# adaLN in a two-layer diffusion block: sums of two column blocks and both conditions on four column parts of TensorE, and the steps around a SwiGLU chunk's end dealt out anew

## The chip, the cores and the metric

The kernel runs on one core of a Trainium2 chip. The metric is the device time of one execution in microseconds, median of several runs. The profile is one further execution; its times count from the first instruction. Engines: PE (TensorE, matmuls; PEld its weight loads), DVE (VectorE), ACT (ScalarE), POOL (GpSimd), SP (SyncE, which here only issues transfers).

## The reference, cut to what matters

```python
def reference(x, c, ctx, c_ctx, ...):          # x 512 x 1024, ctx 256 x 1024
    for i in range(2):
        mod = silu(c) @ w_ada[i] + b_ada[i]        # 1024 -> 6 * 1024, latent tokens
        mod_c = silu(c_ctx) @ w_ada[i] + b_ada[i]  # the same, context tokens
        sh1, sc1, g1, sh2, sc2, g2 = split(mod, 6)
        h = rms_norm(x, norm_mix[i]) * (1 + sc1) + sh1
        y = short_conv(h) if i == 0 else neighbourhood_attention(h, hc)
        x = x + g1 * y
        x = x + g2 * swiglu(rms_norm(x, norm_ffn[i]) * (1 + sc2) + sh2)
        # layer 0 does the same to ctx with mod_c; layer 1 reads ctx and does not update it
    return x

def swiglu(h):                                 # hidden width 2816
    gate, up = split(h @ w_in, 2)
    return (silu(gate) * up) @ w_out
```

Everything is float32. The modulation needs, for each layer, the product of one vector (latent) and, where context is still used, of a second one (context) with a 1024 x 6144 matrix.

## The kernel before

Features lie on the 128 partitions and tokens along the free axis: x is eight tiles of 128 x 512, the context eight of 128 x 256. A product with float32 accuracy is three matmuls: weights and activations are each split into a high and a low part (fp32r), and hi x hi, hi x lo and lo x hi are summed (`mm3`, L186 to L210; its matmuls have line L192). `split` (L136) makes the parts: ACT converts to the high part (L138: wh, ah), DVE subtracts to get the low part (L139: wl, al). `Stream` (L146) loads blocks of 256 weight columns into `raw` and splits them one item ahead of use. `raw` has three buffers, and the blocks of w_ada take theirs from the same three.

The modulation of the columns that the first norm does not need is done by the class `Ada` in the shadow of the big products. Its unit is a step: one half (512 rows) of one block of 512 columns of w_ada. A step loads 1 MB into `raw` (L277) and sums its four 128-row slices, each times its entries of silu(c), into an accumulator `aa` of 128 x 512. For the latent condition DVE does this (L290 the first slice, L292 the others); for the context condition ACT multiplies (L295 the first slice, L298 the others into `pr`) and POOL adds (L299). The context condition is needed for all of layer 0's blocks and for the first four of layer 1's. There are 40 steps; four of them, two column blocks, make one flush: PE sums the accumulators over the 128 partitions (L313), ACT copies the sums from PSUM to `row` (L319), PE transposes them (L322), and DVE adds the bias into `mod` (L328). So there are ten flushes, six with both conditions and four with one.

In the sums of a flush, the column block sets the column part: block j goes to output partitions 32j to 32j + 31. `ones2` holds, for each condition, 32 columns of which one is 1 and the rest 0; the two conditions are accumulated into the same part, one after the other, and come out on two of its rows.

The SwiGLU of layer 0 (`swiglu`, L470) goes through the hidden width in chunks of 6, 8 and 8 tiles. For each hidden tile PE makes gate and up products of x, then of the context; `gate` (L485) forms sg (L489) and splits it into ah and al. Behind the tiles of a chunk comes its output product (`residual`, L449): for each output tile f = 0 to 7 a product over the chunk's hidden tiles for x (18 matmuls in chunk 0) and one for the context (18), each followed by the residual add on DVE (L444). Steps are placed by code: one behind each hidden tile (L551), and in chunks 0 and 1 one behind each of f = 0, 2, 4 of the output product (`also`: flush if four steps are done, then a step), with a flush behind f = 6 (L556).

The order of instructions on each engine is made by a scheduler from estimated times, within the dependences and with the matmuls of sums and transposes pinned in the order of the program. Each engine then runs its own queue in order and waits on semaphores; so an instruction of a step can stand, in DVE's queue, ahead of one that the code wrote earlier.

Of the kernel before, what the change touches and what calls it, by code (L numbers as in the profile page):

```python
# [9 lines left out]
F32 = mybir.dt.float32  # L10
F32R = mybir.dt.float32r
AF = mybir.ActivationFunctionType
ALU = mybir.AluOpType
AX = mybir.AxisListType

P = 128
# [22 lines left out]
def dit_kernel(  # L39
# [16 lines left out]
    nc = tc.nc  # L56
    const = ctx.enter_context(tc.tile_pool(name="const", bufs=1))
# [23 lines left out]
    ident = ct[:, C_ID:C_ID + P]  # L81
# [4 lines left out]
    nc.vector.tensor_copy(out=sel, in_=sel_raw)  # L86
    ones = const.tile([P, 32], F32, name="ones")
    nc.vector.memset(ones, 1.0)
    ones2 = const.tile([P, 2, 32], F32, name="ones2")
    nc.vector.memset(ones2, 0.0)  # L90
    nc.vector.memset(ones2[:, 0, 0:1], 1.0)
    nc.vector.memset(ones2[:, 1, 1:2], 1.0)
    eps = const.tile([P, 1], F32, name="eps")
    nc.vector.memset(eps, EPS)
    pick = const.tile([P, 4], F32, name="pick")
# [26 lines left out]
    def in_order(inst):  # L122
        return tc.keep_in_program_order(inst)
# [89 lines left out]
    class Ada:  # L213
# [90 lines left out]
        def flush(self):  # L304

            if len(self.todo) < 2:
                return
            two, self.todo = self.todo, []
            i, q, both, _ = two[0]
            self.ps = bank("ada", "ada_ps")  # L310
            for c in range(1 + both):
                for j, (_, _, _, accs) in enumerate(two):
                    in_order(nc.tensor.matmul(self.ps[32 * j:32 * j + 32, :], ones2[:, c, :], accs[c],  # L313
                                              start=(c == 0), stop=(c == both)))
            self.finish(i, q // 2)

        def finish(self, i, g):
            row = nrm.tile([P, 512], F32, name="row", tag="row", bufs=1)
            nc.scalar.copy(out=row[0:64, :], in_=self.ps[0:64, :])  # L319
            tp = bank("ada", "ada_tp")  # L320
            for s in range(4):
                in_order(nc.tensor.transpose(out=tp[:, s * 64:(s + 1) * 64], in_=row[0:64, s * P:(s + 1) * P],  # L322
                                             identity=ident[0:64, 0:64]))
            tv = tp[:, 0:256].rearrange("p (s j m) -> p j s m", s=4, j=2)
            ba = vt[:, V_BADA + i * 48 + g * 8:V_BADA + i * 48 + g * 8 + 8].rearrange("p (j s) -> p j s", j=2)
            conds = range(2 if i == 0 or g < 2 else 1)
            for cond in conds:
                nc.vector.tensor_tensor(  # L328
                    out=mod[i][:, cond, g * 8:g * 8 + 8].rearrange("p (j s) -> p j s", j=2),
                    in0=tv[:, :, :, cond], in1=ba, op=ALU.add)  # L330
            if g not in (1, 4):
                return
            which = 0 if g == 1 else 1
            base = V_NMIX if which == 0 else V_NFFN
            gt = const.tile([P, 2, KT], F32, name=f"gain{i}{which}")
            for cond in conds:
                nc.vector.scalar_tensor_tensor(
                    out=gt[:, cond, :], in0=mod[i][:, cond, g * 8:g * 8 + 8], scalar=1.0,
                    in1=vt[:, base + i * KT:base + (i + 1) * KT], op0=ALU.add, op1=ALU.mult)
            gains[(i, which)] = gt  # L340
# [129 lines left out]
    def swiglu(tmp, ap_, i, groups, hs, chunks, ada=None, begin=None, norms=None, out=None, end=None, begin_norm=None):  # L470
# [3 lines left out]
        for ci, n_t in enumerate(chunks):  # L474
            for pr in range(n_t // 2):
                c = (t0 + 2 * pr) * P
                g = block(((ci, pr), "g"), w_in, 0, KT, c)
# [18 lines left out]
        for ci, n_t in enumerate(chunks):  # L496
            srcs = [([], []) for _ in groups]
            tt = 0
            if ci == 0 and begin is not None:
                ws = [st.next() for _ in range(2)]  # L500
                pss, prev = {}, {}

                def in_turn(g):

                    for m in mm3_steps.begun if g in prev else ():
                        behind(m, prev[g])
                    prev[g] = mm3_steps.last

                for g, sub, hooks, hooks3 in begin:
                    c0, c1 = sub.c0, sub.c0 + sub.n  # L510
                    if g not in pss:
                        pss[g] = [bank("mm", "ps") for _ in range(3)]
                    mm3_steps.pin_all = g == 0 and sub.n == NX
                    if len(groups) > 1 and g == 1:
                        begin_norm.apply(hs[1])
                    for part in (((0, 1),) if hooks else ((0,), (1,))):
                        mm3([pss[g][p][:, c0:c1] for p in part], [ws[p] for p in part], *sub.of(hs[g]), hooks)
                    mm3_steps.pin_all = False
                    in_turn(g)
                    if c1 == groups[g].n:  # L520
                        gate(g, pss[g][0], pss[g][1], srcs)
                    if c0 == 0:
                        if len(ws) < 3:
                            ws.append(st.next())
                        grp = groups[g]
                        if grp.n == sub.n:
                            mm3([pss[g][2][:, :grp.n]], [ws[2]], *grp.of(hs[g]), hooks3)
                if begin[0][1].n < groups[0].n:
                    mm3([pss[0][2]], [ws[2]], *groups[0].of(hs[0]))
                if ada is not None:  # L530
                    ada.flush()
                wu = st.next()
                for g, grp in enumerate(groups):
                    pu = bank("mm", "ps")
                    mm3([pu[:, :grp.n]], [wu], *grp.of(hs[g]))
                    gate(g, pss[g][2], pu, srcs)
                tt = 2
                if ada is not None:
                    ada.step(2)
            while tt < n_t:  # L540
                wg, wu = st.next(), st.next()
                for g, grp in enumerate(groups):
                    pg, pu = bank("mm", "ps"), bank("mm", "ps")
                    hi, lo = grp.of(hs[g])
                    mm3([pg[:, :grp.n]], [wg], hi, lo)
                    if ada is not None and g == 0 and tt > 2:
                        ada.flush()
                    mm3([pu[:, :grp.n]], [wu], hi, lo)
                    gate(g, pg, pu, srcs)
                if ada is not None:  # L550
                    ada.step()  # L551
                tt += 1
            last = ci == len(chunks) - 1
            if last and end is not None:
                norms, out = end()
            along = {0: ada.also, 2: ada.also, 4: ada.also, 6: ada.flush} if ada is not None and not last else None  # L556
            residual(st, i, 5, groups, srcs, norms if last else None, out, along=along)


# [1 line left out]
    with ExitStack() as l0:  # L561
# [6 lines left out]
        ada = Ada(tmp, cs)  # L568
# [157 lines left out]
    with ExitStack() as l1:  # L726
# [200 lines left out]
        last, norms = [], []  # L927
# [155 lines left out]
```

## Time and profile before

| | us |
|---|---|
| median of 3 runs | 1640.12 (1639.3 to 1641.58) |
| the profiled execution | 1639.04 |
| its span, first to last instruction | 1637.2 |
| PE busy | 1607.5 (98%) |
| DVE busy | 859.5 (52%) |
| ACT busy | 578.3 (35%) |
| POOL busy | 242.9 (15%) |

1.84 us of the profiled execution lie outside its span. A matmul's row in the timeline gives start and modelled duration, and matmuls are pipelined: the distance between starts, not the duration, is what one costs. The granted clock is 0.998 of full speed over the span. A float32 matmul of the sums is two rows in the trace (two passes).

### The profile page before, as it was taken

The numbers are of one execution on the slowest core, as the hardware profiler recorded it, in microseconds if no ns is written. First come the engines' busy times: TensorE is split into PE (matmuls) and PEld (weight loads), VectorE is DVE, ScalarE is ACT, GpSimd is POOL, SyncE is SP. The second block draws the span as 40 slices with busy tenths as digits, with TensorE's granted clock in tenths as the row PEclk, the third lists the DMA queues.
The fourth block names the chain that finished last, engine by engine and source line by source line (L and its number), as shares of the span: only waits on it lengthen the run. The fifth ranks groups of instructions, "written<-read, shape, count | busy, mean of one in ns | idle before, by whom it ended". The sixth has DMA issues, their size and how long they took to land.

```text
span 1637.2 us, 22217 instructions
## 1 busy us (share of the span) xinstructions
PE 1607.5 (98%) x9156; PEld 1344.5 (82%) x9156; DVE 859.5 (52%) x1393; ACT 578.3 (35%) x967; POOL 242.9 (15%) x290
## 2 busy tenths in 40 slices
PE   6999999999999999999999999999999999999998
PEld 5898888788888888888888777777778788888887
DVE  5567667476654534344423766655677533333333
ACT  4243234354323221122222555555555422222221
POOL 0123226324422000000013201111111000000000
PEclk9999999999999999999999999999999999999999
DMA  9424343134433425133421201111122222323221
GB/s 314 137 78 130 103 154 117 64 122 130 135 127 105 140 93 180 54 127 104 154 68 42 84 27 59 33 59 32 47 71 78 77 98 83 100 81 128 78 84 71
DMA packets 137222, 162.43 MB, mean 99 GB/s; under 512 B 3232, under 2 KB 114208, under 8 KB 137120
## 3 DMA queue, kind: packets, MB, share of 16 engines
q1 hardware_dynamic: 133504, 156.66, 29.4%
q10 hardware_dynamic: 3616, 4.34, 0.8%
q8 instruction: 72, 1.18, 0.3%
q14 instruction: 30, 0.25, 0.0%
HBM read 158.90 MB, written 2.10 MB: 98 GB/s over the span
## 4 chain that ended last, share of the span: by engine, by line
PE 93%; DVE 3%; ACT 1%; DMA 1%; issue 1%; POOL 0%; SPq 0%; POOLq 0%; DVEq 0%; ACTq 0%
PE ps L192 83%; PE op L908 2%; PE tp L898 2%; PE ada_ps L240 1%; PE s L878 1%; DMA raw<-in_w_ada_dram 1%; PE ada_ps L313 1%; PE s L879 1%; PE stt L795 1%; DVE wl L139 1%; DVE t L428 0%; DVE aa L292 0%; PE bc L412 0%; DVE hxl L431 0%; DMA x<-in_xT_dram 0%
## 5 line engine op out<-in xcount | busy, mean ns | idle before, releaser
L192 PE MATMUL ps<-hxh,wh 128*128 128x512 f32 (+1 forms) x1128 | 435.4, 392 | 3.5 <-ACT hxh L430 1.7
L192 PE MATMUL ps<-hxl,wh 128*128 128x512 f32 (+1 forms) x1128 | 431.8, 388 | 1.3 <-DVE hxl L431 1.1
L192 PE MATMUL ps<-hxh,wl 128*128 128x512 f32 (+1 forms) x1128 | 431.1, 388 | 0.5 <-DVE wl L139 0.5
L138 ACT CAST wh<-raw 128x1024 fp32r<-128x1024 f32 (+1 forms) x194 | 198.1, 1022 | 471.4 <-PE ps L192 424.8
L139 DVE TENSOR_TENSOR wl<-raw,wh 128x1024 fp32r<-128x1024 f32 (+1 forms) x194 | 242.1, 1249 | 172.8 <-ACT wh L138 169.0
L192 PEld LDWEIGHTS ps<-hxh,wh 128*128 128x128 f32 x1128 | 210.5, 188 | 53.3 <-issue 4.1
L192 PEld LDWEIGHTS ps<-hxh,wl 128*128 128x128 f32 x1128 | 211.8, 188 | 45.1 <-DVE wl L139 1.4
L192 PEld LDWEIGHTS ps<-hxl,wh 128*128 128x128 f32 x1128 | 211.2, 188 | 43.5 <-DVE hxl L431 3.2
L192 PE MATMUL ps<-ah,wh 128*128 128x512 f32 (+1 forms) x656 | 232.3, 354 | 2.7 <-ACT ah L138 2.7
L192 PE MATMUL ps<-al,wh 128*128 128x512 f32 (+1 forms) x656 | 231.8, 354 | 0.3 <-DVE al L139 0.3
L192 PE MATMUL ps<-ah,wl 128*128 128x512 f32 (+1 forms) x656 | 230.9, 352 | 0.0
L192 PE MATMUL ps<-hch,wl 128*128 128x256 f32 x648 | 181.3, 284 | 0.0
L192 PE MATMUL ps<-hcl,wh 128*128 128x256 f32 x648 | 180.5, 283 | 0.0
L192 PE MATMUL ps<-hch,wh 128*128 128x256 f32 x648 | 179.8, 284 | 0.0
L292 DVE SCALAR_TENSOR_TENSOR aa<-raw,cs,aa 128x512 f32<-128x512 f32 x140 | 144.5, 1033 | 40.9 <-DMA raw<-in_w_ada_dram 37.8
L299 POOL TENSOR_TENSOR aa<-aa,pr 128x512 f32<-128x512 f32 x84 | 135.0, 1608 | 184.3 <-ACT pr L298 111.4
L192 PEld LDWEIGHTS ps<-ah,wh 128*128 128x128 f32 x656 | 123.7, 189 | 25.1 <-issue 3.7
L192 PEld LDWEIGHTS ps<-al,wh 128*128 128x128 f32 x656 | 123.8, 189 | 18.3 <-DVE al L139 0.6
L192 PEld LDWEIGHTS ps<-ah,wl 128*128 128x128 f32 x656 | 123.9, 189 | 17.5
L444 DVE SCALAR_TENSOR_TENSOR x<-ps,mod,x 128x512 f32<-128x512 f32 (+1 forms) x80 | 55.2, 695 | 140.4 <-PE ps L192 140.2
L192 PEld LDWEIGHTS ps<-hch,wh 128*128 128x128 f32 x648 | 122.1, 191 | 4.4 <-issue 1.9
L192 PEld LDWEIGHTS ps<-hcl,wh 128*128 128x128 f32 x648 | 122.8, 191 | 1.9
(172 smaller groups left out, 1595.6 us busy)
## 6 DMA issues: line engine op xcount, KB each, us to landing
raw<-in_ffn_w_in_dram SPq DMA_DIRECT2D x44, 1024.0 KB, 5.1
raw<-in_w_ada_dram SPq DMA_DIRECT2D x40, 1024.0 KB, 5.2
raw<-in_ffn_w_out_dram SPq DMA_DIRECT2D x16, 1024.0 KB, 5.1
raw<-in_attn_w_qkv_dram SPq DMA_DIRECT2D x12, 1024.0 KB, 5.2
raw<-in_conv_w_in_dram SPq DMA_DIRECT2D x9, 1024.0 KB, 5.2
raw<-in_w_ada_dram SPq DMA_DIRECT2D x16, 512.0 KB, 7.9
raw<-in_ffn_w_out_dram SPq DMA_DIRECT2D x8, 768.0 KB, 4.6
raw<-in_conv_w_out_dram SPq DMA_DIRECT2D x4, 1024.0 KB, 5.2
```

What stands on the lines that cost most here:

```text
L138: a = pinned(nc.scalar.copy(out=hi, in_=src))
L139: b = pinned(nc.vector.tensor_tensor(out=lo, in0=src, in1=hi.bitcast(F32), op=ALU.subtract))
L192: m = nc.tensor.matmul(ps, w[k][part], src[k], start=(first and k == i == 0), stop=(last and k == nk - 1 and i == 2))
L240: in_order(nc.tensor.matmul(self.ps[32 * j:32 * j + 32, :wd], self.cs[:, k, :], raw[:, kk, j // 2, j % 2 * wd:(j % 2 + 1) * wd], start=(k ...
L292: nc.vector.scalar_tensor_tensor(out=acc, in0=raw[:, kk, :], scalar=w, in1=acc, op0=ALU.mult, op1=ALU.add)
L299: nc.gpsimd.tensor_tensor(out=acc, in0=acc, in1=pr, op=ALU.add)
L313: in_order(nc.tensor.matmul(self.ps[32 * j:32 * j + 32, :], ones2[:, c, :], accs[c], start=(c == 0), stop=(c == both)))
L444: nc.vector.scalar_tensor_tensor(out=grp.tiles[f], in0=ps, scalar=modv(i, grp.cond, gate, f), in1=grp.tiles[f], op0=ALU.mult, op1=ALU.add)
L795: nc.tensor.matmul(stt[row:row + 32, :], ind, sq, start=True, stop=True)
L878: nc.tensor.matmul(s, qh[a][:, bs], keys(ks[a], w0), start=True, stop=False)
L898: nc.tensor.transpose(out=tp[:, j * P:(j + 1) * P], in_=pt[:, c0:c0 + P], identity=ident)
L908: in_order(nc.tensor.matmul(op_[own, 0:P], vv[:, vi, own], tps[a][:, j * P:(j + 1) * P], start=(j == 0), stop=(j == 3)))
```

## The change

Three things. The sums of a flush go to a column part of their own for each block and condition (four parts with both conditions, two with one), with the plain `ones` as weights and without accumulating; `ones2` and its three memsets go. With both conditions the copy and the four transposes then take 128 rows instead of 64, and the bias add reads the first row of each part. Last, in chunks 0 and 1 the step behind the last hidden tile goes, and the output product has four steps, behind f = 0, 1, 3 and 5, instead of three behind 0, 2 and 4; the last chunk keeps the step behind each tile, and the number and order of steps stay.

```diff
--- before.py
+++ after.py
@@ -86,10 +86,6 @@
     nc.vector.tensor_copy(out=sel, in_=sel_raw)
     ones = const.tile([P, 32], F32, name="ones")
     nc.vector.memset(ones, 1.0)
-    ones2 = const.tile([P, 2, 32], F32, name="ones2")
-    nc.vector.memset(ones2, 0.0)
-    nc.vector.memset(ones2[:, 0, 0:1], 1.0)
-    nc.vector.memset(ones2[:, 1, 1:2], 1.0)
     eps = const.tile([P, 1], F32, name="eps")
     nc.vector.memset(eps, EPS)
     pick = const.tile([P, 4], F32, name="pick")
@@ -308,26 +304,25 @@
             two, self.todo = self.todo, []
             i, q, both, _ = two[0]
             self.ps = bank("ada", "ada_ps")
-            for c in range(1 + both):
-                for j, (_, _, _, accs) in enumerate(two):
-                    in_order(nc.tensor.matmul(self.ps[32 * j:32 * j + 32, :], ones2[:, c, :], accs[c],
-                                              start=(c == 0), stop=(c == both)))
+            for r, acc in enumerate(acc for _, _, _, accs in two for acc in accs):
+                in_order(nc.tensor.matmul(self.ps[32 * r:32 * r + 32, :], ones, acc, start=True, stop=True))
             self.finish(i, q // 2)
 
         def finish(self, i, g):
             row = nrm.tile([P, 512], F32, name="row", tag="row", bufs=1)
-            nc.scalar.copy(out=row[0:64, :], in_=self.ps[0:64, :])
+            nr = P if i == 0 or g < 2 else P // 2
+            nc.scalar.copy(out=row[0:nr, :], in_=self.ps[0:nr, :])
             tp = bank("ada", "ada_tp")
             for s in range(4):
-                in_order(nc.tensor.transpose(out=tp[:, s * 64:(s + 1) * 64], in_=row[0:64, s * P:(s + 1) * P],
-                                             identity=ident[0:64, 0:64]))
-            tv = tp[:, 0:256].rearrange("p (s j m) -> p j s m", s=4, j=2)
+                in_order(nc.tensor.transpose(out=tp[:, s * nr:(s + 1) * nr], in_=row[0:nr, s * P:(s + 1) * P],
+                                             identity=ident[0:nr, 0:nr]))
+            tv = tp[:, 0:4 * nr].rearrange("p (s j c m) -> p j s c m", s=4, j=2, m=32)
             ba = vt[:, V_BADA + i * 48 + g * 8:V_BADA + i * 48 + g * 8 + 8].rearrange("p (j s) -> p j s", j=2)
             conds = range(2 if i == 0 or g < 2 else 1)
             for cond in conds:
                 nc.vector.tensor_tensor(
                     out=mod[i][:, cond, g * 8:g * 8 + 8].rearrange("p (j s) -> p j s", j=2),
-                    in0=tv[:, :, :, cond], in1=ba, op=ALU.add)
+                    in0=tv[:, :, :, cond, 0], in1=ba, op=ALU.add)
             if g not in (1, 4):
                 return
             which = 0 if g == 1 else 1
@@ -547,13 +542,13 @@
                         ada.flush()
                     mm3([pu[:, :grp.n]], [wu], hi, lo)
                     gate(g, pg, pu, srcs)
-                if ada is not None:
+                if ada is not None and (tt < n_t - 1 or ci == len(chunks) - 1):
                     ada.step()
                 tt += 1
             last = ci == len(chunks) - 1
             if last and end is not None:
                 norms, out = end()
-            along = {0: ada.also, 2: ada.also, 4: ada.also, 6: ada.flush} if ada is not None and not last else None
+            along = {0: ada.also, 1: ada.step, 3: ada.also, 5: ada.also, 6: ada.flush} if ada is not None and not last else None
             residual(st, i, 5, groups, srcs, norms if last else None, out, along=along)
```

DVE's queue at the end of chunk 0. First the kernel before: `raw_3971` is the block of the step at f = 0, `raw_4079` that of the step at f = 2 (w_ada); `raw_3789` and `raw_3989` are blocks of w_out for f = 0, 1 and f = 2, 3; sg_3845, al0_3849 belong to the last hidden tile's x columns, sg_3902, al1_3906 to its context columns.

```order
L290 TENSOR_SCALAR aa0_3973<-raw_3971,cs_116 128x512
L292 SCALAR_TENSOR_TENSOR aa0_3973<-raw_3971,cs_116,aa0_3973 128x512 x3
L489 TENSOR_TENSOR sg_3845<-ps_3796,sg_3845 128x512
L292 SCALAR_TENSOR_TENSOR aa0_3973<-raw_4079,cs_116,aa0_3973 128x512
L139 TENSOR_TENSOR al0_3849<-sg_3845,ah0_3848 128x512
L292 SCALAR_TENSOR_TENSOR aa0_3973<-raw_4079,cs_116,aa0_3973 128x512 x2
L139 TENSOR_TENSOR wl_3928<-raw_3789,wh_3927 128x768
L292 SCALAR_TENSOR_TENSOR aa0_3973<-raw_4079,cs_116,aa0_3973 128x512
L489 TENSOR_TENSOR sg_3902<-ps_3853,sg_3902 128x256
L139 TENSOR_TENSOR wl_3992<-raw_3989,wh_3991 128x768
L139 TENSOR_TENSOR al1_3906<-sg_3902,ah1_3905 128x256
```

Then the changed kernel at the same place: `raw_4013` is the block of the step at f = 1, `raw_4121` that of the step at f = 3, `raw_3785`, `raw_3967` the blocks of w_out for f = 0, 1 and f = 2, 3; sg_3841, al0_3845, sg_3898, al1_3902 belong to the last hidden tile.

```order
L286 TENSOR_SCALAR aa0_4015<-raw_4013,cs_112 128x512
L288 SCALAR_TENSOR_TENSOR aa0_4015<-raw_4013,cs_112,aa0_4015 128x512 x3
L484 TENSOR_TENSOR sg_3841<-ps_3792,sg_3841 128x512
L135 TENSOR_TENSOR al0_3845<-sg_3841,ah0_3844 128x512
L135 TENSOR_TENSOR wl_3906<-raw_3785,wh_3905 128x768
L484 TENSOR_TENSOR sg_3898<-ps_3849,sg_3898 128x256
L135 TENSOR_TENSOR wl_3970<-raw_3967,wh_3969 128x768
L135 TENSOR_TENSOR al1_3902<-sg_3898,ah1_3901 128x256
L288 SCALAR_TENSOR_TENSOR aa0_4015<-raw_4121,cs_112,aa0_4015 128x512
L439 SCALAR_TENSOR_TENSOR x0_94<-ps_3909,mod0_91,x0_94 128x512
L288 SCALAR_TENSOR_TENSOR aa0_4015<-raw_4121,cs_112,aa0_4015 128x512 x2
L439 SCALAR_TENSOR_TENSOR c0_102<-ps_3929,mod0_91,c0_102 128x256
```

The four sums of the third step of this group stood between the sg of x and the sg of the context columns; now they stand behind the last al, among the residual adds of the first output tile. Two rows further on follows the split for f = 3 (`raw_3967` for the second time).

SP's queue of transfers at the same place, before (`raw_3767` is the step behind the fifth hidden tile, `raw_3909` the one behind the sixth and last):

```order
L277 DMA raw_3767<-in_w_ada_dram 128x4x512
L159 DMA raw_3789<-in_ffn_w_out_dram 128x6x256
L277 DMA raw_3909<-in_w_ada_dram 128x4x512
L277 DMA raw_3971<-in_w_ada_dram 128x4x512
L159 DMA raw_3989<-in_ffn_w_out_dram 128x6x256
L277 DMA raw_4079<-in_w_ada_dram 128x4x512
L159 DMA raw_4097<-in_ffn_w_out_dram 128x6x256
L277 DMA raw_4201<-in_w_ada_dram 128x4x512
L159 DMA raw_4219<-in_ffn_w_out_dram 128x6x256
```

and in the changed kernel:

```order
L273 DMA raw_3763<-in_w_ada_dram 128x4x512
L155 DMA raw_3785<-in_ffn_w_out_dram 128x6x256
L273 DMA raw_3949<-in_w_ada_dram 128x4x512
L155 DMA raw_3967<-in_ffn_w_out_dram 128x6x256
L273 DMA raw_4013<-in_w_ada_dram 128x4x512
L155 DMA raw_4075<-in_ffn_w_out_dram 128x6x256
L273 DMA raw_4121<-in_w_ada_dram 128x4x512
L155 DMA raw_4183<-in_ffn_w_out_dram 128x6x256
L273 DMA raw_4243<-in_w_ada_dram 128x4x512
```

Two blocks of w_ada in a row have become alternating blocks of w_out and w_ada; each block of w_out from the second on has one block of w_ada less ahead of it.

## Rows read from the trace of the kernel before

**Rows 1.** The chain that ended last, by engine, from the page.
```profile
PE 93%; DVE 3%; ACT 1%; DMA 1%; issue 1%; POOL 0%; SPq 0%; POOLq 0%; DVEq 0%; ACTq 0%
```

**Rows 2.** Timeline, PE, 426 to 451: start, us, engine, line, what [idle before <-releaser].
```profile
426.46 0.39 PE L192 MATMUL ps<-ah,wh 128*128 128x512 f32 x1
...
435.29 0.42 PE L192 MATMUL ps<-ah,wh 128*128 128x256 f32 x1 [2.70 <-ACT ah L138]
...
436.65 0.63 PE L192 MATMUL ps<-ah,wh 128*128 128x512 f32 x1
...
444.00 0.40 PE L192 MATMUL ps<-ah,wh 128*128 128x512 f32 x1
...
450.34 0.39 PE L192 MATMUL ps<-ah,wh 128*128 128x512 f32 x1
```

**Rows 3.** Busy per stretch: us, PE, PEld, DVE, ACT, POOL, then granted clock.
```profile
435.50:438.90 3.40, 3.06 (x9) 2.36 (x9) 2.60 (x5) 0.83 (x1) 0.00 (x0) 0.50 1.02 351
```

**Rows 4.** Timeline, DVE, 417 to 435.
```profile
417.45 3.24 DVE L292 SCALAR_TENSOR_TENSOR aa<-raw,cs,aa 128x512 f32<-128x512 f32 x3
420.98 0.69 DVE L489 TENSOR_TENSOR sg<-ps,sg 128x512 f32<-128x512 f32 x1 [0.28 <-ACT pr L298]
426.07 0.75 DVE L292 SCALAR_TENSOR_TENSOR aa<-raw,cs,aa 128x512 f32<-128x512 f32 x1 [4.40 <-DMA raw<-in_w_ada_dram]
...
427.35 3.49 DVE L292 SCALAR_TENSOR_TENSOR aa<-raw,cs,aa 128x512 f32<-128x512 f32 x2
430.76 2.04 DVE L139 TENSOR_TENSOR wl<-raw,wh 128x768 fp32r<-128x768 f32 x1
...
434.39 0.41 DVE L489 TENSOR_TENSOR sg<-ps,sg 128x256 f32<-128x256 f32 x1
```

**Rows 5.** Timeline, SP (issues of transfers), 411 to 421.
```profile
411.79 0.37 SPq L277 DMA_DIRECT2D raw<-in_w_ada_dram  x1
413.53 0.37 SPq L159 DMA_DIRECT2D raw<-in_ffn_w_out_dram  x1
420.93 0.37 SPq L277 DMA_DIRECT2D raw<-in_w_ada_dram  x1
```

**Rows 6.** Line L277, its 40 transfers: issue to landing.
```profile
DMA to landing us min/median/max: 5.0/5.2/7.5
```

**Rows 7.** Timeline, PE: a flush's sums with both conditions, then with one.
```profile
540.10 1.91 PE L313 MATMUL ada_ps<-aa,ones 128*32 128x512 f32 x8
...
609.46 1.05 PE L313 MATMUL ada_ps<-aa,ones 128*32 128x512 f32 x4
```

**Rows 8.** Timeline, PE: three parts of 512 columns; four parts and full width of 128.
```profile
991.22 0.62 PE L795 MATMUL stt<-sq,ct 128*32 128x512 f32 x2
...
991.69 0.59 PE L795 MATMUL stt<-sqc,ct 128*32 128x512 f32 x1
...
892.52 0.43 PE L397 MATMUL st<-acc,ones 128*32 128x128 f32 x8
...
990.26 1.03 PE L898 MATMUL tp<-ct,pt 128*128 128x128 f32 x8
```

**Rows 9.** Timeline, PE: four transposes of 64 rows, then four of 128.
```profile
546.88 0.39 PE L192 MATMUL ps<-hxh,wh 128*128 128x512 f32 x1
547.20 0.46 PE L322 MATMUL ada_tp<-ct,row 64*128 64x64 f32 x4
...
547.93 0.39 PE L192 MATMUL ps<-hxh,wl 128*128 128x512 f32 x1
...
955.39 0.39 PE L879 MATMUL s<-ks,ql 128*128 128x512 f32 x1
955.63 0.60 PE L898 MATMUL tp<-ct,pt 128*128 128x128 f32 x4
...
956.29 0.39 PE L879 MATMUL s<-ks,ql 128*128 128x512 f32 x1
```

**Rows 10.** Timeline, DVE, first work behind the memsets.
```profile
3.08 0.15 DVE L730 TENSOR_SCALAR vt<-vt 128x1 f32<-128x1 f32 x1 [1.80 <-DMA vt<-in_vec_dram]
```

## The prediction

> **What bounds the kernel now.** I read the page's chain of waits first, then the PE timeline where PE's start-to-start distances jump, then the DVE and SP timelines of the same stretch, then the PE rows of the sums and transposes that the change edits. The reader should see in the chain that PE carries 93% of the span [rows 1]: time is won only by taking instructions off PE or by taking away a wait of PE. DVE, ACT, POOL and the transfers matter only where PE stands waiting for them.
>
> In the PE timeline of layer 0's SwiGLU there is one large wait: the output product of chunk 0 [rows 2]. Each of its eight tiles f is one x product (18 matmuls of 512 columns) and one c product (18 of 256). Undisturbed, such a pair lasts 444.00 to 450.34, 6.34 us. The pair f = 0 lasts 426.46 to 436.65, 10.19 us, and f = 1 lasts 436.65 to 444.00, 7.35 us. So 3.85 + 1.01 = 4.86 us are lost, in two pieces. First PE stands 2.70 us before 435.29, released by ACT's ah: the high half of the hidden tile's c columns is late. Then, between 435.5 and 438.9, the granted clock is 0.50, the 1.2 GHz level; PE had been idle just before [rows 2, 3].
>
> Why ah was late stands in the DVE timeline [rows 4]. DVE runs its queue in order. After sg of the x columns (420.98) comes a sum of the adaLN accumulators that waits 4.40 us for its block of w_ada (426.07), then two more sums at 1.75 us each, a weight split of 2.04 us, and only at 434.39 the sg of the c columns, whose product had been ready since PE turned to the output product at 426.46. The block was issued at 420.93, the moment the sums before it had ended [rows 4, 5]: that step's buffer was the scarce thing. By the order of the kernel before it is the step at f = 2 of the output product; three steps stand there in a row (behind the last tile, at f = 0, at f = 2), and its sum was queued ahead of the last tile's own work.
>
> **The change, part by part.**
>
> (a) The step behind a chunk's last tile goes; four stand at f = 0, 1, 3, 5. In the DVE order of chunk 0's end, the last tile's al, the split of f = 1, sg and al of the c columns and the split of f = 2 now all stand ahead of the waiting sum. Nothing that waits for w_ada is left between them except the sums that stood there already, of the step before. That step's block now goes out in the second slot, 413.53 instead of 411.79 [rows 5], and with the median landing of 5.2 us [rows 6] it is there at 418.7. Its four sums take some 4.3 us (three took 3.24), to 423.0; sg of x 0.69, to 423.7 [rows 4]. With 0.7 us each for ACT's conversion and for al (an estimate, by sg's 0.69) and the slow 2.04 us for the split of f = 1, DVE is at 427.1, a little behind PE's end of the last tile. The sg, split and al of the c columns (0.41, up to 2.04 and some 0.4) end by 430; PE needs them at 432.6 (435.29 less 2.70). Spare: 2.6 us or more. So the wait goes, and with the idle time the half clock behind it: -4.9 us. What is late next: the weights of f = 3, whose split now stands behind the sums of the next step. That step's block waits for the buffer that the split of f = 1 frees (427.1) and lands 5.2 us later, at 432.3; four sums of 0.75 + 3.49 + 1.75 us, two residual adds (1.2, an estimate from a 0.75 us sum and sg's 0.41) and the 2.04 us split end at 441.5. PE comes to f = 3 at 426.46 + 3 x 6.34 = 445.5. Spare: 4.0 us; the slowest landing of a w_ada block in the trace is 7.5 us, 2.3 above the median [rows 6]. Hence nothing is charged here. On SP the transfers of w_out pass two of w_ada; they go out earlier, not later. Chunk 1 has no such wait before, its steps have one condition (DVE alone, no ACT or POOL), and DVE's order has the sums of its last step ahead of the residual add of f = 2, four tiles before the flush: nothing gained or lost.
>
> (b) The sums of two column blocks and both conditions. Before: four matmuls, two column parts, accumulated one condition after the other; eight passes that end 1.91 us after the first starts. The single-condition flush, two parts, has four passes in 1.05 us [rows 7]. So two more stages cost 0.86 us, 0.43 each. After: four matmuls into four parts, none waiting on another. No row has four parts of 512 columns. The bounds: three parts of 512 columns end 1.06 us after their start (991.22 to 992.28), no more than two parts; eight passes of 128 columns in four parts end in 0.43 us, where eight full-width passes of as many columns take 1.03 [rows 8]. The other end is that four parts go no faster than now, 1.91. I take 1.05, by the nearest row (three parts, same columns): 0.86 us saved in each two-condition flush. There are six of these (four in layer 0's blocks, two in layer 1's): -5.2 us. The range for the unknown: -5.2 to 0.
>
> The Trainium skill (TensorE: Matmul & The Clock Gate, "Measured speedup vs the span model") lists only a 2.38-fold speedup for three column parts of 512 columns, and 3.07 for four row parts. By 3.07 the eight passes of 0.43 us would take 1.12 us instead of two stages' 0.86 (an estimate), the saving would be 0.6 us a flush, and the result 1.6 us later than mine, inside the second rival below. The trace does not agree for three parts: their rows lose nothing against two.
>
> (c) The four transposes of a flush take 128 rows instead of 64. From the last full-width start ahead of them to the second matmul behind: 64 rows 546.88 to 547.93, 1.05 us; 128 rows, the attention's own transposes, 955.39 to 956.29, 0.90 us [rows 9]. More columns, but less lost around them. Six times 0.15: -0.9 us. The other end: nothing is won around them and the four take 0.14 us longer (0.60 against 0.46), +0.8 us in all; I take the measured groups.
>
> (d) The copy of the sums out of PSUM has 128 partitions instead of 64 with the same 512 elements each, the adds read with another stride: nothing; ACT's copy is not what PE waits for. The three memsets of ones2 lie before DVE's first wait for a transfer, at 3.08 after 1.80 us idle [rows 10]: nothing.
>
> The sum against the profiled execution: 1639.04 - 4.9 - 5.2 - 0.9 = 1628.0. That execution lies 1.08 us below the median of the runs shown, so 1629.1 for the median.
>
> **Rivals.**
> - A new wait takes the place of the one removed (weights of f = 3, or the next chunk's first split, behind the moved sums). For it: these sums take 1.75 us there, 0.75 at best [rows 4]. Against it: the spares above. It would cost up to what was won in (a): 1629.1 + 4.9 = 1634.0.
> - The fourth part does not run beside three. One more stage of 0.43 us in each of six flushes: 1631.7; no overlap beyond two at all: 1634.3. Against: [rows 8].
> - The change does not do what it says: DVE's wait stays because the block of the step before lands late, and the parts stay in pairs: only (c) remains, 1639.2, no change.
> - Slower: the four parts run one after another, since independent groups into one PSUM bank exclude each other. Eight stages of 0.43 us and 0.2 us of run-in (1.05 less 0.86) make 3.6 us a flush, 1.7 more than now, 10.4 in six: 1629.1 + 5.2 + 10.4 = 1644.7. It decides from 2.9 us a flush on. Against: two and three parts overlap in the rows, and four do at 128 columns.
>
> **How the numbers follow.** Forecast 1629.1, chance 0.80, own range 1627.2 to 1631 (run-to-run spread of some 1 us, and small PE waits elsewhere that shift with the DVE order). New wait 0.09, fourth part not beside three 0.06, no change 0.03, slower 0.02. The range reaches from 1627.2 to 1634.3. About 0.2% (3.3 us) is what a measurement of this kernel can tell from no change. Faster by more: 0.95; within: 0.03; slower: 0.02.
>
> **What would show it.** (a) right: no PE wait over 0.5 us between the last tile and f = 7 of chunk 0, no stretch at 0.50 there, DVE's sg of c ahead of the sum that waits for w_ada. Wrong: PE idle before f = 3 or at the next chunk's first matmul. (b) right: eight passes end about 1.05 us after their start, four starting together. Wrong: a second or third start 0.43 us later in more than two stages. (c) right: 0.9 us from the last full-width start to the second behind. The prediction as a whole is wrong if the time is above 1634.3 or below 1627.2.

## The result, and the profile after

The changed kernel takes 1629.01 us (median of 4 runs, 1626.23 to 1629.3), the kernel before on the same chip 1639.71 (4 runs, 1638.52 to 1641.58). The ratio is 0.9931, 95% interval 0.9916 to 0.9945. The forecast was 1629.1, range 1627.2 to 1634.3. The profiled execution took 1629.08 us with a span of 1627.3, against 1639.04 and 1637.2 before: 9.96 us less, where the sum of the prediction was 11.0.

The chain that ended last, by engine (page of the kernel after; DMA had 1% in [rows 1] and now has 0%):

```profile
PE 95%; DVE 3%; ACT 1%; issue 0%; DMA 0%; SPq 0%; DVEq 0%; ACTq 0%
```

The end of chunk 0 on PE (timeline; the same instructions as [rows 2], with line numbers 4 lower). The first row of a pair is its first x matmul, 426.28 the first context matmul of f = 0:

```profile
422.09 0.39 PE L188 MATMUL ps<-ah,wh 128*128 128x512 f32 x1
...
426.28 0.28 PE L188 MATMUL ps<-ah,wh 128*128 128x256 f32 x1
...
428.41 0.40 PE L188 MATMUL ps<-ah,wh 128*128 128x512 f32 x1
...
434.75 0.39 PE L188 MATMUL ps<-ah,wh 128*128 128x512 f32 x1
...
441.07 0.39 PE L188 MATMUL ps<-ah,wh 128*128 128x512 f32 x1
```

The three pairs take 6.32, 6.34 and 6.32 us, and no row of the stretch has an idle time. From the first row to the last it is 18.98 us; before it was 23.88 (426.46 to 450.34 in [rows 2]). The 4.90 us between them is the whole stall. The granted clock stays at 1.00, where [rows 3] has 0.50 (columns as there; behind the clock stand the busy share of the DMA engines and GB/s):

```profile
426.00:430.00 4.00, 4.00 (x27) 3.63 (x27) 0.51 (x2) 0.35 (x1) 0.00 (x0) 1.00 0.69 250
```

DVE's queue at that place, then SP's (timelines of the kernel after, against [rows 4, 5]):

```profile
416.85 0.49 DVE L286 TENSOR_SCALAR aa<-raw,cs 128x512 f32<-128x512 f32 x1 [3.60 <-DMA raw<-in_w_ada_dram]
417.37 3.24 DVE L288 SCALAR_TENSOR_TENSOR aa<-raw,cs,aa 128x512 f32<-128x512 f32 x3
420.54 0.68 DVE L484 TENSOR_TENSOR sg<-ps,sg 128x512 f32<-128x512 f32 x1
...
424.49 0.41 DVE L484 TENSOR_TENSOR sg<-ps,sg 128x256 f32<-128x256 f32 x1
424.82 0.94 DVE L135 TENSOR_TENSOR wl<-raw,wh 128x768 fp32r<-128x768 f32 x1
425.69 0.41 DVE L135 TENSOR_TENSOR al<-sg,ah 128x256 fp32r<-128x256 f32 x1
429.59 0.75 DVE L288 SCALAR_TENSOR_TENSOR aa<-raw,cs,aa 128x512 f32<-128x512 f32 x1 [3.49 <-DMA raw<-in_w_ada_dram]
...
435.69 2.05 DVE L135 TENSOR_TENSOR wl<-raw,wh 128x768 fp32r<-128x768 f32 x1
```

```profile
411.00 0.37 SPq L273 DMA_DIRECT2D raw<-in_w_ada_dram  x1
420.85 0.37 SPq L155 DMA_DIRECT2D raw<-in_ffn_w_out_dram  x1
424.59 0.37 SPq L273 DMA_DIRECT2D raw<-in_w_ada_dram  x1
```

DVE still waits 3.49 us for a block of w_ada (issued 424.59, there at 429.59), but now the al of the context columns has ended at 426.10 (425.69 + 0.41), ahead of that wait. PE needs it for the last hidden tile of the context product, 15 matmuls of 0.12 us behind 426.28, at 428.1: it is 2 us early.

The sums and transposes of a two-condition flush (after), with the matmuls on either side, and the same sums' neighbours in the kernel before:

```profile
529.53 0.39 PE L188 MATMUL ps<-hxh,wl 128*128 128x512 f32 x1
529.85 1.07 PE L308 MATMUL ada_ps<-aa,ones 128*32 128x512 f32 x8
530.84 0.50 PE L188 MATMUL ps<-hxh,wh 128*128 128x512 f32 x1
...
535.74 0.39 PE L188 MATMUL ps<-hxh,wh 128*128 128x512 f32 x1
535.97 0.60 PE L317 MATMUL ada_tp<-ct,row 128*128 128x128 f32 x4
...
536.64 0.40 PE L188 MATMUL ps<-hxh,wl 128*128 128x512 f32 x1
```

```profile
539.78 0.39 PE L192 MATMUL ps<-hxh,wl 128*128 128x512 f32 x1
...
541.94 0.50 PE L192 MATMUL ps<-hxh,wh 128*128 128x512 f32 x1
```

From neighbour to neighbour the sums take 1.31 us (529.53 to 530.84), before 2.16: 0.85 saved; by durations 1.07 against 1.91 in [rows 7]. The transposes take 0.90 (535.74 to 536.64) against 1.05 in [rows 9].

So the terms measure 4.90 + 6 x 0.85 + 6 x 0.15 = 10.9 us, and the profiled execution is only 9.96 faster. Pairing shows where the rest went. The matmuls of L192 (L188 in the changed kernel) are the same 7536 in each trace, in the same order, so each one's start can be set against its own start in the kernel before; the difference is the lead at that place. The table has the profiled execution of the changed kernel and a second one (the run after_again below):

| place | start before | start after | lead | after_again | lead |
|---|---|---|---|---|---|
| ahead of the first flush with both conditions | 155.15 | 154.82 | 0.33 | 154.22 | 0.93 |
| chunk 0, first x matmul of f = 0 | 426.46 | 422.09 | 4.37 | 421.45 | 5.01 |
| chunk 0, first x matmul of f = 3 | 450.34 | 441.07 | 9.27 | 440.43 | 9.91 |
| behind the last flush with both conditions | 560.07 | 548.77 | 11.30 | 548.12 | 11.95 |
| attention, ahead of a wait of 1.05 us | 960.19 | 949.08 | 11.11 | 948.17 | 12.02 |
| attention, behind it | 990.02 | 978.91 | 11.11 | 979.63 | 10.39 |
| ahead of the second norm of layer 1 | 1267.18 | 1256.04 | 11.14 | 1256.80 | 10.38 |
| behind it | 1276.48 | 1266.52 | 9.96 | 1266.09 | 10.39 |

Between the first row and the fourth, where all three parts of the change lie, the two executions gain 10.97 and 11.02 us, each 4.90 of it in chunk 0. The lead in the first row comes from the start, which differs between executions: the two kernels below that move steps alone, and start as the kernel before does, have 0.97 (154.18) and -0.14 (155.29) there. Behind the parts the first execution loses 1.18 us at the second norm of layer 1, the second 1.63 in the attention. At the norm PE waits 1.30 us in one piece, where the kernel before waits 0.81 and 0.58 in two (at 1270.08 and 1271.88), and a stretch at the 1.2 GHz level follows that the kernel before does not have there: first PE's wait in the timeline, then the stretch.

```profile
1259.42 0.51 PE L188 MATMUL ps<-hxl,wh 128*128 128x256 f32 x2 [1.30 <-DVE hxl L426]
```

```profile
1261.50:1264.90 3.40, 3.40 (x23) 3.02 (x23) 3.05 (x10) 1.85 (x5) 0.00 (x0) 0.50 0.00 0
```

### The profile page after: what moved, and what is told of

It reads as the page before. It is cut to its first block, busy times and chain, and to the rows that moved or that the text cites. A ratio compares the mean times of both kernels' runs of the same rounds, so it can differ in the third digit from the quotient of the medians.

```text
span 1627.3 us, 22211 instructions
## 1 busy us (share of the span) xinstructions
PE 1601.1 (98%) x9156; PEld 1343.9 (83%) x9156; DVE 859.6 (53%) x1390; ACT 577.7 (36%) x967; POOL 242.3 (15%) x290
## 3 DMA queue, kind: packets, MB, share of 16 engines
q8 instruction: 72, 1.18, 0.3%
## 4 chain that ended last, share of the span: by engine, by line
PE 95%; DVE 3%; ACT 1%; issue 0%; DMA 0%; SPq 0%; DVEq 0%; ACTq 0%
PE ps L188 85%; PE op L903 2%; PE tp L893 2%; PE ada_ps L236 1%; PE s L873 1%; PE s L874 1%; PE stt L790 1%; PE ada_ps L308 1%; DVE t L423 0%; DVE hxl L426 0%; PE bc L407 0%; DVE wl L135 0%; PE st L392 0%; DVE acc L380 0%; PE ada_tp L317 0%
## 5 line engine op out<-in xcount | busy, mean ns | idle before, releaser
L188 PE MATMUL ps<-hxh,wh 128*128 128x512 f32 (+1 forms) x1128 | 436.2, 393 | 3.5 <-ACT hxh L425 1.7
L188 PE MATMUL ps<-hxl,wh 128*128 128x512 f32 (+1 forms) x1128 | 432.1, 389 | 1.8 <-DVE hxl L426 1.7
L188 PE MATMUL ps<-hxh,wl 128*128 128x512 f32 (+1 forms) x1128 | 431.7, 388 | 0.5 <-DVE wl L135 0.5
L188 PEld LDWEIGHTS ps<-hxh,wh 128*128 128x128 f32 x1128 | 211.0, 188 | 53.5 <-ACT sg L483 3.4
L188 PEld LDWEIGHTS ps<-hxh,wl 128*128 128x128 f32 x1128 | 212.2, 189 | 45.1 <-DVE wl L135 1.3
L188 PEld LDWEIGHTS ps<-hxl,wh 128*128 128x128 f32 x1128 | 211.7, 188 | 43.9 <-DVE hxl L426 3.5
L188 PE MATMUL ps<-ah,wh 128*128 128x512 f32 (+1 forms) x656 | 231.8, 353 | 0.0
L188 PE MATMUL ps<-al,wh 128*128 128x512 f32 (+1 forms) x656 | 230.8, 352 | 0.0
L188 PE MATMUL ps<-ah,wl 128*128 128x512 f32 (+1 forms) x656 | 230.7, 352 | 0.0
L188 PE MATMUL ps<-hch,wl 128*128 128x256 f32 x648 | 181.3, 284 | 0.0
L188 PE MATMUL ps<-hcl,wh 128*128 128x256 f32 x648 | 180.3, 283 | 0.0
L188 PE MATMUL ps<-hch,wh 128*128 128x256 f32 x648 | 180.0, 284 | 0.0
L188 PEld LDWEIGHTS ps<-ah,wh 128*128 128x128 f32 x656 | 123.4, 188 | 22.0 <-issue 4.6
L188 PEld LDWEIGHTS ps<-al,wh 128*128 128x128 f32 x656 | 123.4, 188 | 17.6
L188 PEld LDWEIGHTS ps<-ah,wl 128*128 128x128 f32 x656 | 123.4, 188 | 17.4
L188 PEld LDWEIGHTS ps<-hch,wh 128*128 128x128 f32 x648 | 122.3, 191 | 4.3 <-issue 1.9
L188 PEld LDWEIGHTS ps<-hcl,wh 128*128 128x128 f32 x648 | 123.0, 191 | 1.8
```

Source lines behind the costliest of these rows:

```text
L188: m = nc.tensor.matmul(ps, w[k][part], src[k], start=(first and k == i == 0), stop=(last and k == nk - 1 and i == 2))
```

## The experiments

In the first four the kernel before ran beside them at 1639.37 us (16 runs, 1637.9 to 1641.52).

**Sums alone.** The changed kernel with four parts and 128-row transposes, but with the steps in their old places:

```diff
-                if ada is not None and (tt < n_t - 1 or ci == len(chunks) - 1):
+                if ada is not None:
                     ada.step()
...
-            along = {0: ada.also, 1: ada.step, 3: ada.also, 5: ada.also, 6: ada.flush} ...
+            along = {0: ada.also, 2: ada.also, 4: ada.also, 6: ada.flush} ...
```

> Sums on four parts and 128-row transposes of the change, steps left in their old places (behind each hidden tile, and f = 0, 2, 4). Theory (the terms add up, each by itself): six flushes x (0.85 + 0.13 us, as the two traces show) = -5.9 us against the kernel before, 1633.8; PE's wait of some 2.7 us before the first output tile's context columns of chunk 0 is still there, and a stretch at granted clock 0.50 behind it. Rival (the sums in pairs made the wait: the accumulators came free late): the wait goes with the sums alone, 1629 to 1630. Rival (the sums gained nothing, all comes from the moved step): 1639 to 1640.

Measured 1635.32 us (9 runs, 1634.0 to 1637.49), ratio 0.9975 (0.9965 to 0.9985): 4.1 us less, not 5.9. The wait is there and longer than before (PE, then DVE, then the window of the clock):

```profile
432.35 0.58 PE L188 MATMUL ps<-ah,wh 128*128 128x256 f32 x1 [4.76 <-ACT ah L134]
```

```profile
423.15 0.75 DVE L288 SCALAR_TENSOR_TENSOR aa<-raw,cs,aa 128x512 f32<-128x512 f32 x1 [5.04 <-DMA raw<-in_w_ada_dram]
```

```profile
430.70:437.50 6.80, 4.96 (x12) 3.85 (x13) 4.47 (x7) 1.68 (x3) 0.28 (x1) 0.50 0.90 296
```

PE stands 4.76 us instead of 2.70, and the stretch at 0.50 lasts 6.80 instead of 3.40; it begins while PE still waits. PE reached the output product 4.99 us earlier than before (421.47 against 426.46). What DVE waits for came only 2.92 us earlier (423.15 against 426.07 in [rows 4]) and the late context matmul 2.94 (432.35 against 435.29 in [rows 2]). DVE's wait, not PE, sets when this matmul starts, so PE's faster sums turned into a longer wait. By f = 3 the lead had shrunk to 2.25 us (448.09 against 450.34); the two flushes behind it added theirs in full. The first theory has the wait right and the time wrong: the sums do gain, but the terms do not simply add while the stall stands. Both rivals fall. Sums and transposes were not run apart; their shares rest on the rows above.

**Step places alone.** The edit above the other way round, on the kernel before: no step behind the last hidden tile in chunks 0 and 1, steps at f = 0, 1, 3, 5, sums in pairs as before.

> Steps at the places of the change, sums in pairs on two parts and 64-row transposes as before. Theory: only the wait in chunk 0 goes, with the half clock behind it: -4.9 us, 1634.8; no PE wait over 0.5 us between 394 and 460 us. Rival (without the shorter sums the wait appears elsewhere, at the weights of f = 3 or the next chunk's first tile): 1637 to 1640.

Measured 1633.84 us (5 runs, 1633.13 to 1634.09), ratio 0.9965 (0.9952 to 0.9979): 5.5 us less. No PE wait over 0.3 us from 390 to 470 us in its trace, and no stretch at 0.50 between the one that begins in the first 25 us, which every trace here has, and the end of the kernel. By pairing, chunk 0 gives 4.90 us (lead 1.02 at 425.44, 5.92 at 444.42). The theory holds; the rival falls. What the medians have beyond 4.9 was not traced to a cause. Alone the two parts give 4.1 + 5.5 = 9.6 us; together they gave 10.7 by the medians of the first result and 12.1 by those of the last four kernels below.

**Another place, with the step behind the last tile kept.** On the kernel before:

```diff
-            along = {0: ada.also, 2: ada.also, 4: ada.also, 6: ada.flush} ...
+            along = {0: ada.flush, 1: ada.step, 3: ada.also, 5: ada.also, 6: ada.flush} ...
```

> The kernel before with its step behind the last hidden tile kept; the steps at f = 0, 2, 4 go to f = 1, 3, 5 instead. Theory (what costs is only that a sum which waits for its block of w_ada stands ahead of the last tile's own sg and al in DVE's queue; here none does, since the step behind the next slot is written later): the wait goes, 1634.8, as with the step dropped. Rival (what costs is a step behind the last tile as such, its transfer and its sums on DVE and POOL at the chunk's end): the wait of 2.7 us and the half clock stay, 1639.7.

Measured 1634.13 us (5 runs, 1633.79 to 1634.33), ratio 0.9967 (0.9954 to 0.9979): 5.2 us less. The runs overlap with those of the kernel that drops the step. DVE's timeline:

```profile
424.84 0.68 DVE L489 TENSOR_TENSOR sg<-ps,sg 128x512 f32<-128x512 f32 x1
...
428.77 0.41 DVE L489 TENSOR_TENSOR sg<-ps,sg 128x256 f32<-128x256 f32 x1
...
429.98 0.41 DVE L139 TENSOR_TENSOR al<-sg,ah 128x256 fp32r<-128x256 f32 x1
434.13 0.75 DVE L292 SCALAR_TENSOR_TENSOR aa<-raw,cs,aa 128x512 f32<-128x512 f32 x1 [3.74 <-DMA raw<-in_w_ada_dram]
```

The sum that waits for w_ada, still 3.74 us, stands behind al, as in the changed kernel. By pairing, chunk 0 gives 4.91 us. So a step behind the last tile costs nothing by itself that these runs can tell; three in a row did, since the third one's sum stood in DVE's queue ahead of the last tile's sg of the context columns and its al.

**The wait without its transfer.** The kernel before, every step in its place in the code; the step at f = 2 of chunk 0 reads a constant tile, and one block of w_ada is left out of the computation:

```diff
+            nc.gpsimd.memset(self.one, 0.01)
...
+            if self.pos == 19:
+                raw = self.one[:, None, :].to_broadcast([P, 4, 512])
+            else:
                 raw = wp.tile([P, 2048], F32, name="raw", tag="raw")
...
```

> The kernel before, every step in its place; the step at f = 2 of chunk 0 reads a constant tile in place of its block of w_ada (one block is left out), so that its four sums stand ahead of the last tile's sg of the context columns as before and wait for no transfer. Theory (the late block is the cause: 4.40 us of DVE's wait): PE's wait before the context columns of f = 0 falls under 0.5 us and no half clock follows, -4.9 us: 1634.8. Rival (DVE's own work ahead of the sg, sums at 1.75 us beside POOL and a split at 2.04 us, is enough to hold PE): a wait of 1 to 2.7 us stays, and with it the half clock, 1637 to 1640.

Measured 1635.56 us (8 runs, 1633.97 to 1636.21), ratio 0.9976 (0.9966 to 0.9986): 3.8 us less. DVE, then PE:

```profile
420.16 6.78 DVE L295 SCALAR_TENSOR_TENSOR aa<-one,cs,aa 128x512 f32<-128x512 f32 x4
426.86 0.68 DVE L492 TENSOR_TENSOR sg<-ps,sg 128x512 f32<-128x512 f32 x1
...
431.00 0.41 DVE L492 TENSOR_TENSOR sg<-ps,sg 128x256 f32<-128x256 f32 x1
...
432.20 0.41 DVE L139 TENSOR_TENSOR al<-sg,ah 128x256 fp32r<-128x256 f32 x1
```

```profile
432.67 0.39 PE L192 MATMUL ps<-al,wh 128*128 128x256 f32 x1 [0.38 <-DVE al L139]
```

All four sums stand ahead of both sg, earlier than in the kernel before, so DVE's order is not the old one; it is harder on the last tile, and still PE waits only 0.38 us, with no stretch at 0.50 behind it. So the late block is the cause, as the theory has it. But al ended at 432.61 and PE took it at 432.67: DVE's own 6.78 us of sums, 1.7 each, had used up the whole margin. By pairing, chunk 0 gives 4.23 us here, not 4.90. Farther on, in the attention, this execution has a stretch at 0.50 behind a wait of 1.05 us; the kernel before passed the same wait (at 968.04) at a clock of 1.00:

```profile
963.28 0.50 PE L881 MATMUL s<-ks,qh 128*128 128x512 f32 x1 [1.05 <-ACT pt L890]
```

```profile
963.70:967.10 3.40, 3.40 (x10) 2.62 (x9) 3.29 (x10) 1.31 (x4) 1.10 (x3) 0.50 0.82 285
```

In this execution the lead falls by 1.60 us there (4.77 at 955.42, 3.17 at 986.85). How much of what 3.8 lacks to 4.9 lies there over all runs stays open.

**The changed kernel again, and three versions of it**, beside the kernel before at 1640.7 us (9 runs, 1638.72 to 1641.63).

> The changed kernel once more, beside the three that follow. Both theories: 1629.0 us, ratio to the kernel before 0.993 to 0.994. If the 1.3 us by which the profiled gain (10.0) fell short of the sum read up to 547 us (11.3) is a stretch of half clock that comes in some executions only, the runs split: those with a mean granted clock of 1.000 lie some 1.4 to 2.8 us below those with 0.997 or 0.998. If it is a lasting wait at the layer-1 norm, all runs agree within 0.5 us whatever their clock.

Measured 1628.57 us (5 runs, 1627.79 to 1628.69), ratio 0.9924 (0.9911 to 0.9938). The runs split by clock: 0.999 in 1627.79 and 1627.87, 0.997 in 1628.57 to 1628.69; the split is 0.8 us, less than the 1.4 expected. In the first result, 1626.23 had 1.000 and 1628.93 to 1629.3 had 0.997 or 0.998. The profile of this execution has no stretch at 0.50 at the layer-1 norm, but one in the attention (PE, then the windows):

```profile
956.02 0.51 PE L873 MATMUL s<-ks,qh 128*128 128x512 f32 x1 [1.05 <-ACT pt L882]
...
957.18 0.63 PE L188 MATMUL ps<-hxl,wh 128*128 128x512 f32 x1
957.61 0.63 PE L188 MATMUL ps<-hxh,wl 128*128 128x512 f32 x1
```

```profile
956.40:959.80 3.40, 3.40 (x10) 2.66 (x9) 3.21 (x10) 1.36 (x4) 1.15 (x3) 0.50 0.83 288
```

In the earlier execution of the same kernel the same wait of 1.05 us was followed by full clock (PE, then the windows):

```profile
956.94 0.50 PE L873 MATMUL s<-ks,qh 128*128 128x512 f32 x1 [1.05 <-ACT pt L882]
```

```profile
956.90:960.30 3.40, 3.36 (x15) 2.79 (x16) 3.37 (x11) 1.78 (x4) 1.31 (x3) 1.00 0.97 313
```

So where the stretch falls differs between executions of one kernel; the table above has what was lost at the place, 1.18 us in the one and 1.63 in the other.

**Four single-condition blocks in one flush.** On the changed kernel; the accumulators of the later blocks take the buffers that the second condition no longer needs, copy and transposes take 128 rows always:

```diff
-            if len(self.todo) < 2:
+            if not self.todo or len(self.todo) < (2 if self.todo[0][2] else 4):
                 return
...
-                self.acc = [... tag=f"aa{c}{q % 2}", bufs=1) for c in range(1 + both)]
+                self.acc = [... tag=f"aa{c if both else q // 2 % 2}{q % 2}", bufs=1) for c in range(1 + both)]
```

> The changed kernel; in addition the single-condition blocks of layer 1 are summed four at a time on four column parts (two flushes of four blocks, not four flushes of two). Theory (four parts of 512 columns cost no more than two, so a flush costs the same whatever it holds): in the changed kernel's trace a single-condition flush adds 1.08 us (sums) and 0.48 us (transposes) to PE, a two-condition one 1.08 and 0.35; 4 x 1.56 - 2 x 1.43 = 3.4 us less: 1625.6. Rival (accumulators that are held longer make the steps late): a new PE or DVE wait, no gain, 1629.

Measured 1625.43 us (4 runs, 1625.22 to 1625.53), ratio 0.9907 (0.9893 to 0.9920); 3.1 us below the changed kernel beside it, and no run of the one in the range of the other. Four blocks cost what four block-and-condition sums cost:

```profile
668.90 0.28 PE L188 MATMUL ps<-ah,wl 128*128 128x256 f32 x1
669.11 1.06 PE L308 MATMUL ada_ps<-aa,ones 128*32 128x512 f32 x8
670.10 0.50 PE L188 MATMUL ps<-ah,wh 128*128 128x512 f32 x1
```

This is the version that beats both kernels. The 3.1 us are a balance. By pairing, the blocks gain 3.9 us, more than expected: the lead goes from 10.60 (549.47) to 14.51 (845.57), while the changed kernel has 11.30 at both places. Its profiled execution also has no stretch at 0.50 in the attention, where after_again's has one. Against that its start was later (lead -0.41 in the first row of the table), and from the last matmul of L188 to the end it took 5.68 us, in the changed kernel 4.59; why was not tried.

**Filling PE's wait at the norm.** On the changed kernel, ten unread matmuls behind the second weight slice:

```diff
+                def fill():
+                    for _ in range(10):
+                        in_order(nc.tensor.matmul(pss[0][2][:, :NX // 2], ws[0][0][0], XA.of(hs[0])[0][0], start=True, stop=True))
...
+                    if len(groups) == 1 and hooks:
+                        hooks = {1: fill, **hooks}
```

> The changed kernel; in addition ten matmuls of 256 columns that nobody reads (they write a bank before its first use) stand in PE's queue at the second norm of layer 1, where PE otherwise waits 1.30 us for the low part of a norm's tile. Theory (PE's standing still there is what the clock answers): no stretch at 0.50 behind it in any run, -1.4 us in those runs that had one: 1627.6, mean granted clock 0.999 or more. Rival (the stretch at 0.50 has to do with something else, such as the small matmuls behind the wait): the stretch stays, 1629, or later by what the ten cost.

Measured 1629.06 us (5 runs, 1627.2 to 1629.29), ratio 0.9927 (0.9914 to 0.9939): no gain on the changed kernel. The ten take the wait's place, the clock there is 1.00, but this execution had its stretch in the attention instead (PE, then the windows):

```profile
956.54 0.50 PE L879 MATMUL s<-ks,qh 128*128 128x512 f32 x1 [1.05 <-ACT pt L888]
...
1258.92 1.36 PE L506 MATMUL ps<-hxh,wh 128*128 128x256 f32 x10
```

```profile
957.20:960.60 3.40, 3.40 (x10) 2.66 (x9) 3.28 (x10) 1.09 (x2) 0.87 (x3) 0.50 0.77 267
1259.00:1266.00 7.00, 6.49 (x69) 5.77 (x68) 5.62 (x16) 4.05 (x11) 2.73 (x3) 1.00 0.00 0
```

As the changed kernel's second profile has full clock there without filling, the run does not tell whether filling prevents the stretch. In these runs filling one wait of several won nothing.

**Both.**

> Flushes of four single-condition blocks and the ten filling matmuls together. If both theories hold and the parts add up: -3.4 - 1.4 = 1624.2. If only the four blocks gain: 1625.6. If neither: 1629.

Measured 1625.21 us (4 runs, 1624.94 to 1625.66), ratio 0.9906 (0.9892 to 0.9920): the same as the four blocks alone. Only the blocks gain: its profiled execution has no stretch at the norm, and the lead is 15.08 us ahead of the norm and behind it (1252.10, 1261.40), so the ten matmuls fill PE's wait and change nothing else.

## Why the prediction was right, point by point

(a) The moved step, -4.9 us: measured 4.90 between the two traces, and 5.5 and 5.2 by the medians of the two kernels that moved steps alone (4.90 and 4.91 in chunk 0). The mechanism is shown from two sides: without the block the stall goes although the sums stand even earlier in DVE's queue, and with every block still loaded, and one of them waited for as long as 3.74 us, it goes once the last tile's work stands ahead of the sums. The prediction counted three sums at and behind the late block; there was a fourth (432.72, 1.75 us), right ahead of the late sg, which changes no term. With the 4.37 us by which the changed kernel is ahead there (422.09 against 426.46), the prediction had the block for f = 1 on chip at 414.3, and the sums began at 416.85; it had al of the context columns ended at 425.6, and that was 426.10. That the second came so close is luck: the block went out at 411.00, 1.84 us later than worked out (409.16), and landed later still, but the two splits took 0.94 us each where up to 2.04 had been charged. PE's spare was 2.0 us, where 2.6 had been worked out. The split for f = 3 ended at 437.74 (435.69 + 2.05) and PE came to f = 3 at 441.07: 3.3 us of spare, 4.0 predicted. The rival that a new wait takes its place did not come about.

(b) Sums on four parts, -5.2 us: 0.85 in the flush shown, 5.1 for six. Four parts of 512 columns take 1.07 us and two take 1.05, and the eight passes start in two groups, four within 0.02 us and four 0.45 later, as the prediction had it. So the rival that the fourth does not run beside three (0.43 more a flush) and the one that parts exclude each other (3.6 us a flush) fall. The Trainium skill (TensorE: Matmul & The Clock Gate, "Measured speedup vs the span model") lists 3.07-fold for four row parts. By it the eight passes had been put 0.26 us above two stages; the trace of these four column parts shows 0.02. (The time that this would have given, 1.6 us above the forecast, lies in the forecast's own range, not in the second rival, which begins at 1631.7.)

(c) The transposes, -0.9 us: 0.90 us from neighbour to neighbour in the flush shown, as the attention's own had it, 0.15 less than before. Together (b) and (c) gain 6.07 and 6.12 us in the two executions of the table outside chunk 0, 1.0 a flush.

(d) Nothing, as costed: no wait of PE falls on the copy or the memsets.

The sum was 11.0; the terms measure 10.9 by their neighbours and 10.97 and 11.02 by pairing. What the sum left out is the clock elsewhere: each of the two profiled executions has a stretch at 0.50 behind another wait, and loses 1.18 or 1.63 us there. That accounts for the 9.96: 0.33 at the start, 10.97 from the change, 0.16 lost on the way and 1.18 at the norm. Runs at a clock of 0.999 or 1.000 were 0.7 to 0.9 us below the others in after_again and 2.7 to 3.1 in the first result; without a trace of those runs, what else they lack stays open. That the median came within 0.1 us of the forecast is therefore partly luck: the starts alone differ by 1.4 us (lead at the first row of the table: -0.41 in the kernel with four blocks, 0.97 in the one with step places alone). The sum was also right for a reason that it did not state. The faster sums alone gain 4.1 us, since the stall eats the rest; only with the stall gone do they bring what (b) and (c) add up to.

## What to carry to other kernels

An in-order queue that mixes urgent work with work that waits for a transfer should have the urgent work written ahead; here it made no difference that the runs could tell whether a step stood behind the last tile, only whether a waiting sum was queued ahead of that tile's own. Before adding up gains, look for a stall whose end is set by another engine: time won ahead of it turns into waiting, and the stall has to go first. Where a change leaves the order of an engine's main work as it was, pairing its instructions between two traces shows where the time was won and where it was lost again. Column parts that stand idle in a reduction are free room: filling four instead of two cost 0.02 us a flush, and the same room took another 3.9 us off PE (3.1 by the medians) when two more blocks were put into it.

## What the runs showed of the hardware that was not expected

- Behind PE waits of 1.05, 1.30 and 2.70 us there was a stretch at 0.50 of 3.40 us; around the wait of 4.76 there was one of 6.80, which began while PE still stood (430.70, PE went on at 432.35). The same wait of 1.05 us in the attention stands in all ten traces: three have the stretch behind it (after_again and the runs with filling and without the transfer), seven full clock. Inside a stretch a 512-column matmul starts every 0.43 us (957.18, 957.61), outside it every 0.23 (18 in 4.19 us from 422.09 to 426.28).
- The same DVE sum took 0.75 us (423.15, 429.59, 434.13) or 1.7 (four in 6.78 at 420.16). In each of the ten traces the 80 or 81 of these 140 sums that no POOL instruction overlaps took at most 0.76 us, and every sum over 1 us overlaps a POOL instruction for 0.73 us or more. No run takes POOL's adds away, so that they are the cause is not shown.
